# Logits of sliding-window softmax attention: two products over 128 rows against three products over 64 rows

## The chip, the cores and the metric

The kernel runs on one core of one Trainium2 chip. The metric is the device time of one execution in microseconds (us). The kernel before was timed three times: 2427.46, 2427.9 and 2433.88 us, median 2427.9 us. One more execution was recorded by the hardware profiler, and all rows of the trace below come from that one.

## The reference, cut to what matters

One decoder layer over 256 positions of width 2048: a SwiGLU feed-forward block, a pair of token mixers (retention and sliding-window softmax attention) fed by one projection, a second feed-forward block, a last RMS norm. The change concerns the logits of the softmax attention alone: 32 query heads of width 64, 8 key heads (four query heads share one), window and block of 128 positions.

```python
def swa_with_sinks(q, k, v, sinks):
    ...
    logits = jnp.einsum('bnqhgd,bnkhd->bnhgqk', qb, kb).astype(jnp.float32) * (d ** -0.5)
    ...
    logits = jnp.where(valid[None, :, None, None], logits, NEG_INF)
    ...
    probs = jax.nn.softmax(jnp.concatenate([logits, sink], axis=-1), axis=-1)[..., :-1]
    out = jnp.einsum('bnhgqk,bnkhd->bnqhgd', probs.astype(v.dtype), vb)
    return out.reshape(b, s, hq * d)
```

## The kernel before, in words

All large products are done in fp32r on TensorE with each operand split in two parts, a rounded part ("hi", written by a ScalarE cast) and what is left over ("lo", a VectorE subtraction). A product of activations and weights is three matmuls (lines 348 to 350): hi with hi, lo with hi, hi with lo, each 128 x 512 outputs wide. They go into the accumulators called `pa`. The weights arrive by DMA as `raw` and are split into `wh` and `wl` at lines 356 and 357.

The token mixing goes over the projection `w_in` in chunks of 512 columns (`in_chunk`). While the three matmuls of a chunk run, side work is fed between them: after every quarter of a chunk `gemm` calls `step()`, which advances a list `side` of generators by one. Softmax attention is such side work. A generator `window(pair)` handles two query heads (a pair); there are 16 pairs. Its first half is `window_weights` (logits, mask, exponentials), its second half `window_values` for the pair before (transposes of the weights, line 1251, and the products with the values, line 1267).

What the logits read is made ahead of them. `keys` holds, for each of the eight key heads, the hi part and the lo part with the head's 64 numbers twice, on partitions 0 to 63 and again on 64 to 127. `queries` holds for each pair two forms, one for each head: the head's hi part on its own half of the partitions, its lo part on the other half (lines 1316 to 1322, two ScalarE casts and two VectorE subtractions of 64 x 512 for each of two row blocks in each of four chunks). So one matmul over 128 partitions against hi keys gives hi times hi plus lo times hi, and a second against lo keys gives hi times lo plus lo times lo.

`window_weights` (from line 1189) writes the two heads' logits of the second row block, which see 256 keys, into one PSUM bank, and those of the first row block, which see 128 keys, into a second bank: eight matmuls for a pair (line 1202), four of 256 columns and four of 128. VectorE then reads the first bank once (line 1209, times the mask `pick`), adds two halves (line 1210), and reads the second bank once (line 1211). The banks come from the pool `psd` (`side_bank`), which has two.

The order of the instructions on TensorE, VectorE and ScalarE in this stretch is not the order of the code: a scheduler sets it from the dependencies and its own model of durations. The engines then work through their lists strictly in that order.

Of the kernel before, what the change touches and what calls it, by code (L numbers as in the profile page):

```python
# [9 lines left out]
F32 = mybir.dt.float32  # L10
F32R = mybir.dt.float32r
AF = mybir.ActivationFunctionType
ALU = mybir.AluOpType
# [3 lines left out]
P = 128  # L17
S = 256
# [12 lines left out]
QH, KVH, HD = 32, 8, 64  # L31
# [46 lines left out]
def layer_kernel(  # L78
# [22 lines left out]
    nc = tc.nc  # L101
# [16 lines left out]
    def nm(s):  # L118
        uid[0] += 1
        return f"{s}_{uid[0]}"  # L120
# [4 lines left out]
    def bank():  # L125
        return psm.tile([P, CH], F32, tag="ps", name=nm("ps"))

    def side_bank():
        return psd.tile([P, CH], F32, tag="pd", name=nm("pd"))

    def t512():
        return tmp.tile([P, CH], F32, tag="t512", name=nm("t"))
# [7 lines left out]
    def small(n, tag):  # L140
        return two.tile([P, n], F32, tag=tag, name=nm(tag))
# [218 lines left out]
    def pair_tile():  # L360
        return asp.tile([P, 2, CH], F32, tag="a", name=nm("a"))
# [46 lines left out]
    def gemm(act, w, col0s, KT=KD, ready=None):  # L408
        banks = [[acc_bank() for _ in range(NT)] for _ in col0s]
        for kb in range(KT // KB):  # L410
            gemm_part(act, w, col0s, banks, kb, KT, ready if kb == 0 else None)
            step()
        return banks
# [454 lines left out]
    banks, moved = {}, set()  # L868
# [104 lines left out]
    with tc.manual_schedule(engines=ORDERED):  # L973
# [21 lines left out]
        for _ in range(3):  # L995
# [8 lines left out]
            out=s2, in_=ssq.rearrange("p (t i) -> p t i", t=NT), axis=AX.X, op=ALU.add  # L1004
        )
        nc.vector.tensor_scalar(
            out=v2, in0=s2, scalar1=1.0 / D, scalar2=EPS, op0=ALU.mult, op1=ALU.add
# [6 lines left out]
            out=q2, in0=q2, scalar1=-0.5, scalar2=1.5, op0=ALU.mult, op1=ALU.add  # L1014
# [85 lines left out]
    for g, ks in enumerate(groups):  # L1100
# [7 lines left out]
        for i, n in enumerate(order):  # L1108
            if i < first_i:
                continue  # L1110
            at = i - first_i
# [25 lines left out]
    def in_chunk(c0, ready=None):  # L1137
        return gemm(held, wi, [c0], ready=ready)[0]
# [10 lines left out]
    keys = one.tile([P, 2, KVH, S], F32R, tag="x", name="keys")  # L1149
    b = in_chunk(O_SV, ready)  # L1150
    for t in range(NT):
        for g in range(2):
# [8 lines left out]
            for j in range(4):  # L1161
                js = slice(j * P, (j + 1) * P)
                nc.tensor.transpose(ps[:, js], kd[:, js], ident)
            hi, lo = (
                keys[:, i, g * 4 : g * 4 + 4, t * P : (t + 1) * P] for i in range(2)
            )
            p4 = ps.rearrange("p (h s) -> p h s", h=4)
# [5 lines left out]
    for t in range(NT):  # L1173
# [4 lines left out]
    queries = [  # L1178
        v.rearrange("p (j a s) -> p j a s", j=4, a=2)
        for v in (homes[:, : KD * P], other, homes[:, : KD * P], homes[:, KD * P :])  # L1180
    ]
# [3 lines left out]
    pick, causal, own = masks[:, : 2 * P], masks[:, 2 * P : 3 * P], masks[:, 3 * P :]  # L1185

    def twice(v):
        return v[:, None, :].broadcast_to([P, 2, v.shape[1]])

    def window_weights(pair):  # L1190


        kv = pair // 2
        both = pair_tile()
        lg, parts = both[:, :, :S], both[:, :, S:]
        banks = [side_bank(), side_bank()[:, :S]]
        of_t = [v.rearrange("p (i s) -> p i s", i=2) for v in banks][::-1]
        for i in range(2):
            qs = queries[pair // 4][:, pair % 4, i, :]
            for t in (1, 0):  # L1200
                for n in range(2):
                    nc.tensor.matmul(  # L1202
                        of_t[t][:, i, :],
                        qs[:, t * P : (t + 1) * P],
                        keys[:, n, kv, : (t + 1) * P],
                        start=n == 0,
                        stop=n == 1,
                    )
        nc.vector.tensor_mul(parts, of_t[1], twice(pick))
        nc.vector.tensor_add(lg[:, :, :P], parts[:, :, :P], parts[:, :, P:])  # L1210
        nc.vector.scalar_tensor_tensor(
            out=lg[:, :, P:], in0=of_t[0], scalar=HD**-0.5, in1=twice(causal),
            op0=ALU.mult, op1=ALU.add,
        )
        mx = small(4, "mx")
        m2 = mx.rearrange("p (i t) -> p i t", t=2)
        nc.vector.tensor_reduce(
            out=m2, in_=lg.rearrange("p i (t s) -> p i t s", t=2), axis=AX.X, op=ALU.max
        )
        sb = sink_b[:, 2 * pair : 2 * pair + 2]  # L1220
        nc.vector.tensor_tensor(
            out=m2, in0=m2, in1=sb[:, :, None].broadcast_to([P, 2, 2]), op=ALU.max
        )
        ng = small(4, "ng")
        nc.vector.tensor_scalar(out=ng, in0=mx, scalar1=-1.0, scalar2=None, op0=ALU.mult)
        se = small(4, "se")
        nc.vector.tensor_tensor(
            out=se.rearrange("p (i t) -> p i t", t=2),
            in0=ng.rearrange("p (i t) -> p i t", t=2),
            in1=sb[:, :, None].broadcast_to([P, 2, 2]),  # L1230
            op=ALU.add,
        )
        nc.scalar.activation(se, se, AF.Exp)
        sm = small(4, "sm")
        for i in range(2):
            for z in (2 * i, 2 * i + 1):
                seg = lg[:, i, z % 2 * P : (z % 2 + 1) * P]
                nc.scalar.activation(
                    seg, seg, AF.Exp, bias=ng[:, z : z + 1], accum_out=sm[:, z : z + 1]
                )  # L1240
        nc.vector.tensor_add(sm, sm, se)
        nc.vector.reciprocal(sm, sm)
        return lg, sm
# [46 lines left out]
    def window(pair):  # L1290
        held_lg = window_weights(pair)
        if pair > 4 and pair % 4 == 1:
            window_out(pair // 4 - 1)
        yield
        if before:
            window_values(*before.pop())
        before.append((pair, *held_lg))
        if pair == QH // 2 - 1:
            yield
            window_values(*before.pop())  # L1300
            yield
            window_out(pair // 4)
        yield

    for ci in range(4):
        b = in_chunk(O_SQ + ci * CH)
        for t in range(NT):
            u = t512()
            nc.any.tensor_copy(u, b[t])
            ps = bank()  # L1310
            for j in range(4):
                js = slice(j * P, (j + 1) * P)
                nc.tensor.transpose(ps[:, js], u[:, js], ident)
            q4 = queries[ci]
            p4 = ps.rearrange("p (j s) -> p j s", j=4)
            for a in range(2):
                here, there = (slice(c * HD, (c + 1) * HD) for c in (a, 1 - a))
                hi = q4[here, :, a, t * P : (t + 1) * P]
                nc.scalar.copy(hi, p4[here])
                nc.vector.tensor_sub(  # L1320
                    q4[there, :, a, t * P : (t + 1) * P], p4[here], hi.bitcast(F32)
                )
        side += [window(pair) for pair in range(ci * 4, ci * 4 + 4)]


# [1 line left out]
    for a, off in ((0, O_RQ), (1, O_RK)):  # L1327
        for ci in range(2):
            b = in_chunk(off + ci * CH)
            for t in range(NT):  # L1330
                u = t512()
                v = t512()
                p4 = b[t].rearrange("p (h a d) -> p h a d", h=4, a=2)
# [107 lines left out]
    for p in range(2):  # L1441
        sg = first if p == 0 else gates(p)
        c0s = [(2 * p + i) * CH for i in range(2)]
        for g, a, w in ((1, a_swa, w_swa_branch), (0, a_ret, w_ret_branch)):
            banks = gemm(a, w[0], c0s)
# [109 lines left out]
```

## Time and profile before

| | us |
|---|---|
| median of three timed runs | 2427.9 |
| lowest, highest | 2427.46, 2433.88 |
| the profiled execution, as timed | 2425.96 |
| its span, first to last instruction | 2424.2 |
| TensorE matmul busy in the span | 2394.7 |
| VectorE, ScalarE busy | 1707.3, 1182.5 |

An engine's busy time is the time in which at least one of its instructions is running. Matmuls overlap in the pipeline, so the duration of one matmul (0.39 us for 512 columns) is longer than the distance between the starts of two that follow each other; what a matmul costs in a stream is read from the starts. Weight loads (PEld) are recorded apart from the matmuls (PE). Where the records show two matmuls starting within 0.03 us of each other, the next distance is longer, and only the sum over such a place can be used.

### The profile page before, as it was taken

How to read it: one execution, taken by the hardware profiler on the slowest of the kernel's cores; microseconds unless marked ns; L12 is line 12 of the kernel's file. 1: busy time of each engine (PE TensorE's matmuls, PEld its weight loads, DVE VectorE, ACT ScalarE, POOL GpSimd, SP SyncE). 2: the span in 40 equal slices, each digit the busy share in tenths (PEclk: the TensorE clock that was granted, in tenths of full speed). 3: DMA queues.
4: the chain of work that ended last, by engine and by line, in shares of the span. 5: the costliest groups of instructions: out<-in, count | busy, mean ns of one | idle time of the engine just before them, and what ended most of it. 6: DMA issues, size and time to landing. Idle time of an engine off the chain costs nothing.

```text
span 2424.2 us, 28881 instructions
## 1 busy us (share of the span) xinstructions
PE 2394.7 (99%) x10916; PEld 1981.0 (82%) x10916; DVE 1707.3 (70%) x2497; ACT 1182.5 (49%) x1596; POOL 8.3 (0%) x19
## 2 busy tenths in 40 slices
PE   7999999999999999999999999999999999999998
PEld 5887888888888888888888788888888888888886
DVE  7878787778877688886666776768565555545656
ACT  6644554444546455454444444456444444444544
POOL 0000000000000000000000000000000000000000
PEclk9999999999999999999999999999999999999999
DMA  9887678888876666566677777755666666665563
GB/s 372 329 300 302 210 273 334 333 315 319 309 287 217 242 223 224 209 244 209 243 261 255 248 260 272 266 191 191 211 242 224 226 226 235 234 224 191 185 199 122
DMA packets 244543, 603.32 MB, mean 249 GB/s; under 512 B 9810, under 2 KB 10194, under 8 KB 224818
## 3 DMA queue, kind: packets, MB, share of 16 engines
q1 hardware_dynamic: 242850, 591.61, 68.6%
q0 software_dynamic: 1552, 9.87, 1.0%
q8 instruction: 85, 1.39, 0.2%
q14 instruction: 56, 0.45, 0.1%
HBM read 597.22 MB, written 4.22 MB: 248 GB/s over the span
## 4 chain that ended last, share of the span: by engine, by line
PE 95%; DMA 2%; DVE 2%; issue 0%; ACT 0%; SPq 0%; DVEq 0%; ACTq 0%
PE pa L350 28%; PE pa L349 28%; PE pa L348 28%; DMA slot<-in_w_ada_dram 2%; PE pa L724 1%; PE ps L466 1%; PE pd L348 1%; PE pd L350 1%; PE pd L349 1%; PE pd L1267 1%; PE pd L1202 1%; DVE wl L357 0%; PE pd L1251 0%; DMA x_sb<-in_x_dram 0%; DVE slot L227 0%
## 5 line engine op out<-in xcount | busy, mean ns | idle before, releaser
L357 DVE TENSOR_TENSOR wl<-raw,wh 128x1024 fp32r<-128x1024 f32 (+1 forms) x784 | 942.2, 1206 | 591.2 <-ACT wh L356 587.0
L356 ACT CAST wh<-raw 128x1024 fp32r<-128x1024 f32 (+1 forms) x784 | 815.0, 1040 | 1025.7 <-PE pa L349 972.3
L348 PE MATMUL pa<-wh,hh 128*128 128x512 f32 x2014 | 788.4, 391 | 0.9 <-ACT wh L356 0.9
L349 PE MATMUL pa<-wh,hl 128*128 128x512 f32 x2014 | 786.8, 391 | 0.0
L350 PE MATMUL pa<-wl,hh 128*128 128x512 f32 x2014 | 726.8, 392 | 0.0
L348 PEld LDWEIGHTS pa<-wh,hh 128*128 128x128 f32 x2014 | 378.2, 188 | 78.7 <-ACT wh L356 1.3
L349 PEld LDWEIGHTS pa<-wh,hl 128*128 128x128 f32 x2014 | 378.2, 188 | 76.9
L350 PEld LDWEIGHTS pa<-wl,hh 128*128 128x128 f32 x2014 | 376.2, 188 | 76.2
L349 PE MATMUL pa<-wh,a 128*128 128x512 f32 x992 | 384.2, 389 | 1.2 <-DVE a L389 1.2
L348 PE MATMUL pa<-wh,a 128*128 128x512 f32 x992 | 367.2, 390 | 1.1 <-ACT wh L356 0.9
L350 PE MATMUL pa<-wl,a 128*128 128x512 f32 x992 | 367.0, 390 | 0.6 <-DVE wl L357 0.6
L348 PEld LDWEIGHTS pa<-wh,a 128*128 128x128 f32 x992 | 185.9, 188 | 41.4 <-ACT wh L356 1.8
L349 PEld LDWEIGHTS pa<-wh,a 128*128 128x128 f32 x992 | 186.2, 188 | 40.6 <-DVE a L389 2.1
L350 PEld LDWEIGHTS pa<-wl,a 128*128 128x128 f32 x992 | 185.8, 188 | 40.2 <-DVE wl L357 1.9
L227 DVE CUSTOM_DVE_ANT_0 slot<-slot,cact 128x1024 f32<-128x1024 f32 (+1 forms) x126 | 182.4, 1475 | 18.9 <-DMA slot<-in_w_ada_dram 18.7
L227 DVE CUSTOM_DVE_ANT_0 raw<-raw,cact 128x512 f32<-128x512 f32 (+1 forms) x260 | 166.9, 695 | 24.0 <-DMA raw<-in_w_ada_dram 22.9
L389 DVE TENSOR_TENSOR a<-slot,a 128x512 fp32r<-128x512 f32 x124 | 84.8, 685 | 4.9 <-ACT a L388 4.9
L388 ACT CAST a<-slot 128x512 fp32r<-128x512 f32 x124 | 76.4, 618 | 5.3 <-PE pa L350 5.2
L467 ACT COPY slot<-ps 128x512 f32<-128x512 f32 x75 | 41.4, 586 | 35.2 <-PE ps L466 35.0
L348 PE MATMUL pd<-wh,hh 128*128 128x512 f32 x144 | 56.1, 391 | 1.1 <-DVE slot L947 1.1
L349 PE MATMUL pd<-wh,hl 128*128 128x512 f32 x144 | 56.1, 390 | 0.0
L350 PE MATMUL pd<-wl,hh 128*128 128x512 f32 x144 | 51.2, 392 | 0.0
(237 smaller groups left out, 1398.7 us busy)
## 6 DMA issues: line engine op xcount, KB each, us to landing
raw<-in_w_ffn_gu_dram SPq DMA_DIRECT2D x148, 1024.0 KB, 4.9
raw<-in_w_in_dram SPq DMA_DIRECT2D x104, 1024.0 KB, 5.1
raw<-in_w_ffn_down_dram SPq DMA_DIRECT2D x88, 1024.0 KB, 5.0
slot<-in_w_ada_dram SPq DMA_DIRECT2D x78, 1024.0 KB, 7.6
raw<-in_w_ada_dram SPq DMA_DIRECT2D x64, 1024.0 KB, 4.8
raw<-in_w_ffn_gu_dram SPq DMA_DIRECT2D x25, 768.0 KB, 7.5
raw<-in_w_swa_branch_dram SPq DMA_DIRECT2D x16, 1024.0 KB, 5.1
raw<-in_w_ret_branch_dram SPq DMA_DIRECT2D x16, 1024.0 KB, 5.2
```

What stands on the lines that cost most here:

```text
L227: nc.vector.tensor_tensor_reduce(out=w[:, at], in0=w[:, at], in1=cact[:, at], scale=1.0, scalar=0.0, op0=ALU.mult, op1=ALU.add, accum_out= ...
L348: nc.tensor.matmul(ps, ah[:, j, ts], wh[:, j, :], start=first, stop=False)
L349: nc.tensor.matmul(ps, al[:, j, ts], wh[:, j, :], start=False, stop=False)
L350: nc.tensor.matmul(ps, ah[:, j, ts], wl[:, j, :], start=False, stop=last)
L356: nc.scalar.copy(hi, src)
L357: nc.vector.tensor_sub(lo, src, hi.bitcast(F32))
L388: nc.scalar.copy(hi, v)
L389: nc.vector.tensor_sub(lo, v, hi.bitcast(F32))
L466: nc.tensor.transpose(ps[:, j * P : (j + 1) * P], src_of(j), ident)
L467: nc.any.tensor_copy(dest, ps[:, : n * P])
L724: nc.tensor.matmul(banks[t], a[:, j, t * P : (t + 1) * P], wt[:, j, :], start=(kb, hs[0], n) == (0, 0, 0), stop=(kb, hs[-1], n) == (KD // ...
L1202: nc.tensor.matmul(of_t[t][:, i, :], qs[:, t * P : (t + 1) * P], keys[:, n, kv, : (t + 1) * P], start=n == 0, stop=n == 1,)
```

## The change

The logits of a head become three matmuls over that head's 64 partitions: hi queries with hi keys, lo with hi, hi with lo. The product lo with lo is no longer formed. The heads of a pair sit on opposite halves of the partitions and are written by turns in the code; each head gets a PSUM bank of its own, 256 columns for the second row block and 128 beside them for the first. A pair has twelve matmuls instead of eight. VectorE reads each bank twice, so four instructions instead of two. The queries are stored as a hi tile and a lo tile, each over all 128 partitions: one cast and one subtraction of 128 x 512 where there were two of each of 64 x 512.

```diff
-        banks = [side_bank(), side_bank()[:, :S]]
-        of_t = [v.rearrange("p (i s) -> p i s", i=2) for v in banks][::-1]
+        banks = [side_bank() for _ in range(2)]
+        terms = ((0, 0), (1, 0), (0, 1))
+        for t, at in ((1, slice(0, S)), (0, slice(S, S + P))):
+            for n, (of_q, of_k) in enumerate(terms):
+                for i in range(2):
+                    here = slice(i * HD, (i + 1) * HD)
+                    nc.tensor.matmul(
+                        banks[i][:, at],
+                        queries[pair // 4][here, pair % 4, of_q, t * P : (t + 1) * P],
+                        keys[here, of_k, kv, : (t + 1) * P],
+                        start=n == 0,
+                        stop=n == len(terms) - 1,
+                    )
         for i in range(2):
-            qs = queries[pair // 4][:, pair % 4, i, :]
-            for t in (1, 0):
-                for n in range(2):
-                    nc.tensor.matmul(
-                        of_t[t][:, i, :],
-                        qs[:, t * P : (t + 1) * P],
-                        keys[:, n, kv, : (t + 1) * P],
-                        start=n == 0,
-                        stop=n == 1,
-                    )
-        nc.vector.tensor_mul(parts, of_t[1], twice(pick))
+            nc.vector.tensor_mul(parts[:, i, :], banks[i][:, :S], pick)
+            nc.vector.scalar_tensor_tensor(
+                out=lg[:, i, P:], in0=banks[i][:, S : S + P], scalar=HD**-0.5, in1=causal,
+                op0=ALU.mult, op1=ALU.add,
+            )
         nc.vector.tensor_add(lg[:, :, :P], parts[:, :, :P], parts[:, :, P:])
-        nc.vector.scalar_tensor_tensor(
-            out=lg[:, :, P:], in0=of_t[0], scalar=HD**-0.5, in1=twice(causal),
-            op0=ALU.mult, op1=ALU.add,
-        )
...
-            for a in range(2):
-                here, there = (slice(c * HD, (c + 1) * HD) for c in (a, 1 - a))
-                hi = q4[here, :, a, t * P : (t + 1) * P]
-                nc.scalar.copy(hi, p4[here])
-                nc.vector.tensor_sub(
-                    q4[there, :, a, t * P : (t + 1) * P], p4[here], hi.bitcast(F32)
-                )
+            hi, lo = (q4[:, :, a, t * P : (t + 1) * P] for a in range(2))
+            nc.scalar.copy(hi, p4)
+            nc.vector.tensor_sub(lo, p4, hi.bitcast(F32))
```

The scheduler's order on TensorE, at the first pair. `pd` is a side bank, `pa` an accumulator of the projection; L1202 is the logits' line in both kernels, and 128x256 or 128x128 is the size of the output. Before, in a row:

```order
L349 MATMUL pa_6438<-wh_6543,hl_4048 128x512
L1202 MATMUL pd_6477<-keys,homes_6263 128x256 x2
L1202 MATMUL pd_6478<-keys,homes_6263 128x128 x2
L350 MATMUL pa_6437<-wl_6544,hh_4047 128x512
L350 MATMUL pa_6438<-wl_6544,hh_4047 128x512
```

And after, ten of the pair's twelve, where pd_6473 is the bank of the first head and pd_6474 that of the second:

```order
L349 MATMUL pa_6434<-wh_6545,hl_4048 128x512
L1202 MATMUL pd_6473<-keys,homes_6263 128x256
L1202 MATMUL pd_6474<-keys,homes_6263 128x256
L1202 MATMUL pd_6473<-keys,homes_6263 128x256
L1202 MATMUL pd_6474<-keys,homes_6263 128x256
L1202 MATMUL pd_6473<-keys,homes_6263 128x128
L1202 MATMUL pd_6474<-keys,homes_6263 128x128
L1202 MATMUL pd_6473<-keys,homes_6263 128x128
L1202 MATMUL pd_6474<-keys,homes_6263 128x128
L1202 MATMUL pd_6473<-keys,homes_6263 128x128
L1202 MATMUL pd_6474<-keys,homes_6263 128x128
L350 MATMUL pa_6433<-wl_6546,hh_4047 128x512
```

Here the halves do alternate; the same holds, with two doubled rows, for the second pair.

TensorE again, at the third pair, the second of its two runs of logits. Before:

```order
L348 MATMUL pa_6684<-wh_6823,hh_4047 128x512
L349 MATMUL pa_6684<-wh_6823,hl_4048 128x512
L1202 MATMUL pd_6722<-keys,homes_6263 128x128 x4
L350 MATMUL pa_6684<-wl_6824,hh_4047 128x512
L348 MATMUL pa_6683<-wh_6871,hh_4047 128x512
L349 MATMUL pa_6683<-wh_6871,hl_4048 128x512
```

After (L1252 is the transposes of `window_values`, line 1251 before):

```order
L349 MATMUL pa_6687<-wh_6833,hl_4048 128x512
L350 MATMUL pa_6687<-wl_6834,hh_4047 128x512
L1202 MATMUL pd_6726<-keys,homes_6263 128x256 x3
L1202 MATMUL pd_6726<-keys,homes_6263 128x128 x3
L1252 MATMUL pd_6797<-small_c,a_6578 128x128 x4
L348 MATMUL pa_6688<-wh_6833,hh_4047 128x512
```

Before, a run is one row block of both heads; after, a run is all six matmuls of one head, in one bank and on one half of the partitions, and the other head's six stand 30 rows further up. From the third pair to the sixteenth the two heads' runs stay apart in this way, by other distances, and two of the 28 runs are cut into five and one. With the three runs of the first two pairs (2, 10 and 12 matmuls) that makes 33 runs; before there are 34, all but four of them of four matmuls.

VectorE at the third pair, before:

```order
L1209 TENSOR_TENSOR a_6720<-pd_6721,slot_6259 128x2x256
L1320 TENSOR_TENSOR other<-ps_6674,other 64x4x128
L1210 TENSOR_TENSOR a_6720<-a_6720 128x2x128
L357 TENSOR_TENSOR wl_6889<-raw_6869,wh_6888 128x1024
L1320 TENSOR_TENSOR other<-ps_6663,other 64x4x128
L1320 TENSOR_TENSOR other<-ps_6674,other 64x4x128
L1211 SCALAR_TENSOR_TENSOR a_6720<-pd_6722,slot_6259 128x2x128
```

After:

```order
L1210 TENSOR_TENSOR a_6724<-pd_6725,slot_6259 128x256
L1319 TENSOR_TENSOR other<-ps_6680,other 128x4x128
L1211 SCALAR_TENSOR_TENSOR a_6724<-pd_6725,slot_6259 128x128
L357 TENSOR_TENSOR wl_6888<-raw_6885,wh_6887 128x1024
L357 TENSOR_TENSOR wl_6905<-raw_6885,wh_6904 128x1024
L1210 TENSOR_TENSOR a_6724<-pd_6726,slot_6259 128x256
L1211 SCALAR_TENSOR_TENSOR a_6724<-pd_6726,slot_6259 128x128
```

The reading of a bank is split by heads, and the queries' subtraction (L1320 before, L1319 after) stands half as often.

## Rows read from the trace of the kernel before

**Rows 1.** The page, busy time of each engine over the span
```profile
PE 2394.7 (99%) x10916; PEld 1981.0 (82%) x10916; DVE 1707.3 (70%) x2497; ACT 1182.5 (49%) x1596; POOL 8.3 (0%) x19
```

**Rows 2.** Windows: stretch, length, busy us (instructions) by engine, clock, DMA share, GB/s
```profile
845.00:1095.00 250.00, 250.00 (x1340) 213.74 (x1339) 206.34 (x437) 128.84 (x273) 1.59 (x3) 1.00 0.63 222
```

**Rows 3.** Timeline, TensorE: start, us, engine, line, operation, tiles, shapes, count
```profile
857.47 0.39 PE L349 MATMUL pa<-wh,hl 128*128 128x512 f32 x1
857.69 0.63 PE L1202 MATMUL pd<-keys,homes 128*128 128x256 f32 x4
858.16 0.39 PE L350 MATMUL pa<-wl,hh 128*128 128x512 f32 x1
858.39 0.40 PE L348 MATMUL pa<-wh,hh 128*128 128x512 f32 x1
```

**Rows 4.** Timeline, TensorE, around four logits of 128 columns
```profile
862.49 0.56 PE L1202 MATMUL pd<-keys,homes 128*128 128x128 f32 x4
862.89 0.45 PE L349 MATMUL pa<-wh,hl 128*128 128x512 f32 x1
863.17 0.62 PE L350 MATMUL pa<-wl,hh 128*128 128x512 f32 x2
```

**Rows 5.** Timeline, weight loads and matmuls of the three start-up transposes
```profile
9.81 0.18 PEld L200 LDWEIGHTS ps<-small_c,t 48*128 48x128 f32 x1 [3.67 <-DMA small_c<-in_consts_dram]
10.07 0.18 PEld L201 LDWEIGHTS ps<-small_c,t 128*128 128x128 f32 x1
10.48 0.18 PEld L202 LDWEIGHTS ps<-small_c,t 16*128 16x128 f32 x1 [0.22 <-issue]
...
10.08 0.47 PE L201 MATMUL ps<-small_c,t 128*128 128x128 f32 x1
10.48 0.28 PE L202 MATMUL ps<-small_c,t 16*128 16x16 f32 x1
```

**Rows 6.** Timeline, TensorE, two transposes of one shape
```profile
18.14 0.77 PE L899 MATMUL ps<-small_c,t 128*128 128x128 f32 x2 [2.26 <-ACT t L892]
```

**Rows 7.** Timeline, TensorE, around a transpose with 16 output rows
```profile
451.17 0.39 PE L349 MATMUL pa<-wh,hl 128*128 128x512 f32 x1
451.40 0.27 PE L291 MATMUL ps<-small_c,modc 128*16 128x128 f32 x1
451.42 0.71 PE L350 MATMUL pa<-wl,hh 128*128 128x512 f32 x2
451.97 0.40 PE L348 MATMUL pa<-wh,hh 128*128 128x512 f32 x1
```

**Rows 8.** Groups by shape: count, busy us, mean ns, idle before; or ns min/median/max
```profile
L1209 DVE TENSOR_TENSOR a<-pd,slot 128x512 f32<-128x512 f32 x16 | 11.0, 687 | 0.4
L1211 DVE SCALAR_TENSOR_TENSOR a<-pd,slot 128x256 f32<-128x256 f32 x16 | 6.8, 422 | 6.3 <-PE pd L1202 6.2
L1320 DVE TENSOR_TENSOR homes<-ps,homes x12: 683/686/694, 843.2 to 942.5; 64x512 fp32r<-64x512 f32 x12
L1320 DVE TENSOR_TENSOR other<-ps,other x4: 684/686/694, 878.5 to 882.8; 64x512 fp32r<-64x512 f32 x4
L389 DVE TENSOR_TENSOR a<-slot,a 128x512 fp32r<-128x512 f32 x124 | 84.8, 685 | 4.9 <-ACT a L388 4.9
L1319 ACT CAST homes<-ps x12: 579/581/584, 842.6 to 941.4; 64x512 fp32r<-64x512 f32 x12
L1319 ACT CAST other<-ps x4: 579/582/586, 877.9 to 880.6; 64x512 fp32r<-64x512 f32 x4
```

**Rows 9.** Timeline, start: matmuls over one row, and their weight loads
```profile
4.53 0.62 PE L188 MATMUL pa<-c,ones 1*128 1x512 f32 x1
4.95 0.62 PE L189 MATMUL pa<-c,ones 1*128 1x512 f32 x1
...
4.53 0.33 PEld L189 LDWEIGHTS pa<-c,ones 1*128 1x128 f32 x1
4.96 0.33 PEld L188 LDWEIGHTS pa<-c,ones 1*128 1x128 f32 x1
```

## The prediction

> **What bounds the kernel now.** I read the page first. TensorE is busy for 2394.7 of 2424.2 us [rows 1], which alone says little, since a busy matmul row need not be a row at full pace. So I took the windows of the stretch in which the change works: the first logits start at 850, the last values end near 1089 us, and from 845 to 1095 TensorE is busy for 250.00 of 250 us at a granted clock of 1.00, the 2.4 GHz level, VectorE for 206.34, ScalarE for 128.84 [rows 2]. The reader is to see that nothing else ever holds TensorE up there: what the change costs or saves on TensorE moves the end one for one, and what it does on VectorE and ScalarE has 43.7 and 121.2 us of idle time to disappear in. The third view was the timeline of TensorE alone, because it gives the distance between starts, which is what a matmul costs in a stream.
>
> **What a small matmul costs.** Matmuls of 512 columns start 0.23 us apart. Four logits matmuls of 256 columns stand between two of them: they start at 857.69, the next large one at 858.16, and it is followed at the usual distance [rows 3]. So the four cost 0.47 us, 0.118 each. Four of 128 columns take 0.40 to the next start, and that next one then takes 0.28 in place of 0.23, so 0.45 in all, 0.113 each [rows 4]. Half the columns save almost nothing: both run at the pace at which weights are loaded, not at that of the columns.
>
> **Part 1, the count.** Before: 16 pairs with four of either kind, 16 x (0.47 + 0.45) = 14.7 us. After: six of either kind per pair, 96 x 0.118 + 96 x 0.113 = 22.2 us, if a matmul over 64 rows costs what one over 128 costs. It does unless its weights load faster, and the start-up transposes show loads of 48, 128 and 16 rows that all take 0.18 us [rows 5]. I take +7.4 us. From below: if half the rows loaded in half the time, the 128-column ones would be bound by their columns, 0.23 x 128/512 = 0.057 us, and the sum would be 96 x 0.118 + 96 x 0.057 = 16.8, +2.1 us.
>
> **Part 2, opposite halves.** The code alternates the halves, so that two heads could stream at once. But the order, which the scheduler sets, does so for two pairs of sixteen; in the other fourteen a run is six matmuls of one head on one half, and the other head's run stands some large matmuls away. So at most 24 matmuls can overlap, worth at most 12 x 0.115 = 1.4 us. No row of before has two halves at work. Bounds 0 and -1.4, I take the middle, -0.7.
>
> **Part 3, changing the shape of the array's use.** Each of the 33 runs now stands between instructions over 128 rows, so TensorE goes from 128 rows to 64 and back 66 times; before never, in this stretch. What does a change cost? The nearest rows are the start-up transposes. The 128-row one starts at 10.08, the 16-row one at 10.48, 0.40 apart, and the weight load of the second sat idle for 0.22 us behind nothing that the profile shows, until just before the first was done [rows 5]. Two transposes of one shape, at the same slow pace, start 0.77 - 0.47 = 0.30 apart [rows 6]. So the change cost 0.10 there. The other way: in the middle of the full-pace stream, a transpose with 16 output rows goes by between 128-row matmuls; from 451.17 to 451.97 there are three 512-column matmuls (3 x 0.23) and it, so it cost 0.11, what a small matmul costs anyway, and nothing for the change [rows 7]. That one changes the columns of the array in use, not its rows. Bounds per change: 0 by that row, 0.22 by the idle load. I take 0.10, the row that changes rows as this kernel does, unhalved although the start-up runs at the slower pace (0.42 us per 512 columns [rows 9]), since it does not show what the time consists of: 66 x 0.10 = +6.6 us; ends 0 and 14.5.
>
> The Trainium skill says in TensorEngine Tiling (Array Packing), under Key Properties, that changing the tiling mode, not just the tile, drains the TensorE; it gives no time. The start-up transposes [rows 5] agree with it and the 16-row one [rows 7] does not: with it the sum has the term of part 3, without it the sum stops at part 1 and 2.
>
> **Part 4, VectorE and ScalarE.** Reads of the banks: before 687 + 422 ns a pair. After, two of 128 x 256 at 422 and two of 128 x 128, which by the same slope (265 ns per 256 columns) I estimate at 290: 1424 ns, +0.32 us a pair, +5.0 us. The queries: 16 subtractions of 64 x 512 at 686 ns become 8 of 128 x 512, and half as many partitions were not cheaper: line 389 takes 685 on 128 [rows 8]. So -5.5 us on VectorE, and 8 casts of 0.58 less on ScalarE, -4.7 us. The net, near zero and negative, lies under TensorE's 250 us without a gap. If that cover went, it would be through a bank: with two side banks, head two's run, or the transposes after it, wait for VectorE to have read the other bank, twice now. The six waits of VectorE for the logits (6.3 us in all [rows 8]) say that VectorE comes to the bank first as often as not. I take 0, and allow +2 us; a matmul that waits in TensorE's list holds up all large ones behind it.
>
> **The sum.** 7.4 - 0.7 + 6.6 = +13.3 us on the profiled execution, 2425.96 + 13.3 = 2439.3, its 1.8 us outside the span unchanged. The median of the runs shown is 1.9 us above that execution, so 2427.9 + 13.3 = 2441.2; I forecast 2441. With 0.05 to 0.22 us per change, and part 2 between its ends, it is +9 to +22, 2437 to 2450.
>
> **The rivals.**
> *A change of rows is free.* Then +6.0 to +7.4 us, 2434 to 2435. For it the 16-row transpose in the stream [rows 7], against it the start-up [rows 5]; it decides below some 0.02 us per change. This lies just under 0.3%, which is 7.3 us and about what a measurement of this kernel tells from none.
> *Not slower: half-height weights load in half the time, and a change is free.* The mechanism sits in the 96 matmuls of 128 columns, whose price falls from 0.113 to 0.057. Then +2.1 - 0.7 = +1.4, with the 256-column ones still at 0.118; 2429. Against it the equal loads [rows 5], taken at the slow pace where something else might set 0.18. It decides from a price below about 0.08 for each.
> *The halves do run side by side everywhere*, as the change says: 192 matmuls in 96 places, 96 x 0.115 = 11.0 against 14.7, -3.7 us, 2424. The order speaks against it, since the runs of the two halves are large matmuls apart. Even then it stays within 0.3%; faster by more would need half of the 14.7 us to go.
> *Loads on one half do not run ahead.* If in a run on one half each weight load waits for the matmul before it, every logits matmul bears a load in the open. What that is worth: after the transpose the two matmuls of line 350 take 451.42 to 451.97, 0.55 for 2 x 0.23, so 0.09 [rows 7]. 192 x 0.09 = 17 more, +31 us, 2459. Against it: the start-up matmuls over a single row have their next load start together with the matmul before it, and keep an even 0.42 apart [rows 9]. The Trainium skill has the rule for it in TensorE: Matmul & The Clock Gate, Part 3, The mechanism: a load overlaps a matmul in flight only where the row group differs. These loads [rows 9] and all of the 128-row stream contradict it.
>
> **How the numbers follow.** Forecast 0.56; change free 0.20; half-time loads 0.12; side by side 0.04; loads in the open 0.08. Slower by over 0.3%: the forecast, the last rival, and a third of the free change, since its upper end sits on the line: 0.70 in round numbers. Faster by over 0.3%: 0.02, for something in the fourth that I do not see. Within: 0.28. The range 2430 to 2452 holds the forecast with its ends and 2 us of bank waits, and the free change; it leaves out the loads in the open, the side by side, and half of the half-time loads. The forecast's own range is 2437 to 2450.
>
> **What would show it.** In the profile after: 192 matmuls on line 1202, their six-runs 0.69 us long from start to start plus some 0.1 at either side; the weight load of each run's first matmul, and that of the first large one after it, starting late by that much; TensorE's stretch of side work longer by 13 us, with the stages before and after it unchanged; alternate starts within a few hundredths only in the first two pairs. I am wrong if the six-runs are bordered at the ordinary 0.23 us, if six take much less than 0.69, or if TensorE waits for a side bank.

## The result, and the profile after

The changed kernel takes 2450.03 us (median of six runs, 2445.09 to 2453.46) against 2430.7 us for the kernel before (six runs): a ratio of 1.0081, 95% interval 1.0069 to 1.0092, or +17 to +22 us of 2430. The forecast was 2441, slower, in a range from 2430 to 2452.

The profiled execution of the changed kernel took 2452.41 us, at the upper end of its runs, and part of the 26 us between the two profiled executions lies outside the change. So I compare inside the stretch, between two large matmuls, one ahead of the first logits and one behind the last, with the same other matmuls between them in both kernels. Before, then after:

```profile
847.63 0.39 PE L349 MATMUL pa<-wh,hl 128*128 128x512 f32 x1
1097.39 0.40 PE L349 MATMUL pa<-wh,hl 128*128 128x512 f32 x1
...
853.57 0.39 PE L349 MATMUL pa<-wh,hl 128*128 128x512 f32 x1
1119.94 0.39 PE L349 MATMUL pa<-wh,hl 128*128 128x512 f32 x1
```

The stretch grows from 249.8 to 266.4 us, by 16.6. Of the rest, 5.9 us lie ahead of it and 4 behind. There the execution after shows TensorE idle for 1.6 us and a clock of 0.83 from 205 to 215 us, and the same idle time and a clock of 0.79 from 1363 to 1371; that of before shows no idle time and 1.00 in both windows.

The page's first row, and the same stretch by windows, as [rows 1, 2] for before:

```profile
PE 2416.2 (99%) x10980; PEld 1991.6 (81%) x10980; DVE 1702.4 (69%) x2520; ACT 1179.3 (48%) x1589; POOL 8.3 (0%) x19
```
```profile
845.00:1115.00 270.00, 270.00 (x1423) 224.35 (x1422) 204.42 (x464) 127.64 (x269) 1.58 (x3) 1.00 0.60 209
```

64 matmuls more, VectorE and ScalarE a little less busy, and TensorE again without an idle moment at a granted clock of 1.00. What grew is the time between its starts. The timeline of TensorE (start, duration, line, operation, tiles, shapes, count), first at the second pair, whose twelve matmuls go by turns, then at the second head of the third pair, six on one half; and under it the weight loads of the latter moment:

```profile
862.80 0.39 PE L350 MATMUL pa<-wl,hh 128*128 128x512 f32 x1
863.12 0.90 PE L1202 MATMUL pd<-keys,homes 64*128 64x256 f32 x12
863.96 0.49 PE L348 MATMUL pa<-wh,hh 128*128 128x512 f32 x1
864.29 0.39 PE L349 MATMUL pa<-wh,hl 128*128 128x512 f32 x1
...
887.82 0.39 PE L349 MATMUL pa<-wh,hl 128*128 128x512 f32 x1
888.04 0.39 PE L350 MATMUL pa<-wl,hh 128*128 128x512 f32 x1
888.36 0.90 PE L1202 MATMUL pd<-keys,homes 64*128 64x256 f32 x6
889.19 0.66 PE L1252 MATMUL pd<-small_c,a 128*128 128x128 f32 x4
```
```profile
887.82 0.19 PEld L350 LDWEIGHTS pa<-wl,hh 128*128 128x128 f32 x1
888.36 0.75 PEld L1202 LDWEIGHTS pd<-keys,homes 64*128 64x128 f32 x6 [0.35 <-issue]
889.19 0.42 PEld L1252 LDWEIGHTS pd<-small_c,a 128*128 128x128 f32 x4
```

In the stream, the weights of a matmul are loaded while the one before it runs. Here the load for the first logits sits idle for 0.35 us behind "issue", which is nothing that the profile shows, and starts only at 888.36, together with its matmul, 0.32 after the start of the last large one instead of 0.23. The six take 0.83 us to the next start, where 0.69 was worked out; all 26 runs of six take 0.82 to 0.84. The twelve by turns take 0.84, no longer than six on one half, and the large matmul after them 0.33 in place of 0.23. So a run costs 0.09 ahead of it, 0.14 within and 0.10 behind, some 0.34 us over its places of 0.115 each; and two matmuls on opposite halves share one place. VectorE's reads came out as estimated [rows 8], the 128-column one at 279 ns where I had 290:

```profile
L1210 DVE TENSOR_TENSOR a<-pd,slot 128x256 f32<-128x256 f32 x32 | 13.4, 419 | 6.7 <-PE pd L1202 6.6
L1211 DVE SCALAR_TENSOR_TENSOR a<-pd,slot 128x128 f32<-128x128 f32 x32 | 8.9, 279 | 0.0
```

### The profile page after: what moved, and what is told of

Read it like the earlier page. It is cut to its first block, busy times and chain, and to the rows that moved or that the text cites. A ratio compares the mean times of both kernels' runs of the same rounds, so it can differ in the third digit from the quotient of the medians.

```text
span 2450.6 us, 29039 instructions
## 1 busy us (share of the span) xinstructions
PE 2416.2 (99%) x10980; PEld 1991.6 (81%) x10980; DVE 1702.4 (69%) x2520; ACT 1179.3 (48%) x1589; POOL 8.3 (0%) x19
## 4 chain that ended last, share of the span: by engine, by line
PE 94%; DMA 3%; DVE 2%; issue 1%; ACT 0%; SPq 0%; DVEq 0%; ACTq 0%
PE pa L350 28%; PE pa L349 28%; PE pa L348 28%; DMA slot<-in_w_ada_dram 2%; PE pa L724 1%; PE ps L466 1%; PE pd L348 1%; PE pd L349 1%; PE pd L350 1%; PE pd L1202 1%; PE pd L1268 1%; DVE wl L357 1%; PE pd L1252 0%; DMA x_sb<-in_x_dram 0%; DMA raw<-in_w_ada_dram 0%
```

## The experiments

The theory: 33 runs x 0.34 + 192 x 0.115 - 12 shared places x 0.115 = 31.9 us where there were 14.7, +17 us. All differences below are the measured ratio less one, times 2430 us, with the interval. In some places the trace of the one profiled execution is added, as the time between two large matmuls, one ahead of the first logits and one well behind the last (847.63 and 1164.09 us before), with the same other matmuls between them in every kernel; I call this the long stretch.

**1. All 128 rows, everything else left.** Both heads get the sum of the two heads' logits.

```diff
-                    here = slice(i * HD, (i + 1) * HD)
+                    here = slice(0, P)
```

> The changed kernel with all twelve logits matmuls of a pair over 128 partitions in place of 64 (so each head gets the sum of both heads' products; the order of the instructions, the banks, the reads and the query split stay those of the changed kernel, word for word). Theory (border): what the change costs beyond its 64 more matmuls is paid where TensorE goes from 128 rows to 64 and back, about 0.34 us per run of logits; without the 64 rows only the count is left, 64 x 0.115 = +7.4 us against the kernel before, about 2438, and the six-runs sit 0.69 us from start to start with 0.23 at either side. Rival (reads and order): the rest comes from the split reads, the banks or the new order; then it stays near +19, about 2450.

Measured: ratio 1.0031 (1.0020 to 1.0041), +7.5 us (4.9 to 10.0). The same order, banks, reads and query split as the changed kernel, row for row, and two thirds of the loss are gone. A six-run of it and what follows:

```profile
908.62 0.40 PE L349 MATMUL pa<-wh,hl 128*128 128x512 f32 x1
908.86 0.80 PE L1202 MATMUL pd<-keys,other 128*128 128x256 f32 x6
909.49 0.44 PE L350 MATMUL pa<-wl,hh 128*128 128x512 f32 x1
909.77 0.39 PE L348 MATMUL pa<-wh,hh 128*128 128x512 f32 x1
```

It starts 0.24 after the large matmul and takes 0.63, the next 0.28: 0.69 us above the stream, against 1.03. The count is worth 7.5 us and the 64 rows the rest. The rival, reads and order, is out.

**2. Two terms, so eight matmuls as before, on 64 rows.** The product of lo queries and hi keys is left out.

```diff
-        terms = ((0, 0), (1, 0), (0, 1))
+        terms = ((0, 0), (0, 1))
```

> The changed kernel without the product of lo queries and hi keys: eight matmuls per pair as in the kernel before, each over 64 rows (28 runs of four on one half, two runs of eight by turns). Theory (border): a run costs 0.34 + 0.115 per place, 30 x (0.34 + 4 x 0.115) = 24.0 us against 14.7 before, +9.3 us, about 2440; a four-run and its borders take 0.80 us. Rival (per matmul): each 64-row matmul costs 0.17 wherever it stands, as the six-runs' 1.03 us divided by six; then a four-run with its borders takes 0.68, and the sum is +5.7, about 2436. Rival (count alone): no change against before, about 2430.

Measured: 1.0033 (1.0020 to 1.0046), +8.0 us (4.9 to 11.2). With no matmul added it is slower, so count alone falls. The times don't part the other two (9.3 and 5.7 both lie inside), the trace does:

```profile
911.61 0.39 PE L350 MATMUL pa<-wl,hh 128*128 128x512 f32 x1
911.92 0.68 PE L1202 MATMUL pd<-keys,other 64*128 64x256 f32 x4
912.53 0.50 PE L348 MATMUL pa<-wh,hh 128*128 128x512 f32 x1
912.86 0.39 PE L349 MATMUL pa<-wh,hl 128*128 128x512 f32 x1
```

0.08 ahead, 0.61 for the four, 0.10 behind: 0.79, where the price per run says 0.80 and the price per matmul 0.68.

**3. By turns for every pair.** The twelve are chained, and their banks come from two pools where both are free at once.

```diff
-        banks = [side_bank() for _ in range(2)]
+        banks = [bank(), acc_bank()]
...
+                    if last is not None:
+                        tc.add_manual_dep(mm.ins, last.ins.name, ...)
+                    last = mm
```

> The changed kernel with the twelve matmuls of each pair chained so that they issue by turns on the two halves, and with the two banks taken from the transposes' pool and the accumulators' pool, so that 18 runs are left, 16 whole twelves but for two that are cut. Theory (border and overlap): two matmuls on opposite halves share one place; 18 x 0.34 + 96 x 0.115 = 17.2 us against 14.7 before, +2.5 us, about 2433; a twelve-run takes 0.84 us from its start to the next. Rival (no overlap; the fast twelve-run of the profile is an accident of its place): 18 x 0.34 + 192 x 0.115 = 28.2, +13.5 us, about 2444.

Measured: 1.0014 (1.0003 to 1.0025), +3.4 us (0.7 to 6.1), as the theory has it. Here the two banks have different names, so the timeline keeps the matmuls apart (from the start of a run on; `ps` and `pa` are the two heads' banks):

```profile
888.11 0.40 PE L350 MATMUL pa<-wl,hh 128*128 128x512 f32 x1
888.43 0.38 PE L1203 MATMUL ps<-keys,homes 64*128 64x256 f32 x1
888.44 0.38 PE L1203 MATMUL pa<-keys,homes 64*128 64x256 f32 x1
888.66 0.27 PE L1203 MATMUL ps<-keys,homes 64*128 64x256 f32 x1
888.66 0.27 PE L1203 MATMUL pa<-keys,homes 64*128 64x256 f32 x1
888.77 0.28 PE L1203 MATMUL ps<-keys,homes 64*128 64x256 f32 x1
...
889.26 0.50 PE L348 MATMUL pa<-wh,hh 128*128 128x512 f32 x1
```

The two heads start within 0.01 us of each other. The first place takes 0.22 and those after it 0.11: the load in the open at the head of a run is to be seen here by itself.

**4. The order and banks of 3, both heads on the lower half.** The second head of a pair gets the first one's logits.

```diff
-                    here = slice(i * HD, (i + 1) * HD)
+                    here = slice(0, HD)
```

> As the kernel by turns with 18 runs, same order and same banks, but both heads read the lower half of the partitions (so the second head of a pair gets the first one's logits). Theory (overlap needs opposite halves): each matmul has a place of its own, 18 x 0.34 + 192 x 0.115 = 28.2 us, +13.5 against before, about 2444, 11 us above the kernel by turns; a twelve-run takes about 1.5 us. Rival (it is the alternation of the two banks that lets matmuls overlap): as the kernel by turns, about 2433.

Measured: 1.0045 (1.0031 to 1.0058), +10.9 us (7.5 to 14.1). A run of twelve, its start and what follows it:

```profile
888.53 0.38 PE L1203 MATMUL ps<-keys,homes 64*128 64x256 f32 x1
888.75 0.28 PE L1203 MATMUL pa<-keys,homes 64*128 64x256 f32 x1
888.87 0.28 PE L1203 MATMUL ps<-keys,homes 64*128 64x256 f32 x1
888.99 0.28 PE L1203 MATMUL pa<-keys,homes 64*128 64x256 f32 x1
...
889.85 0.27 PE L1203 MATMUL pa<-keys,homes 64*128 64x128 f32 x1
890.05 0.43 PE L1278 MATMUL pd<-slot,t 128*128 128x64 f32 x2
```

1.52 us against 0.83: opposite halves let two matmuls share a place, not two banks. Within the run starts are 0.11 to 0.12 apart, the pace of full-height matmuls.

**5. By turns, with the banks left in the side pool.** The edit of 3 without its first line.

> The changed kernel with the twelve matmuls of a pair chained by turns, and its two banks left in the side pool: the first matmul of most pairs then goes alone and eleven follow, 35 runs in place of 18, with nearly the same sharing of places. Theory (border, 0.34 us per run): against the kernel by turns with 18 runs 17 more runs, +5.8 us, and some six places lost where a lone matmul has no partner, +0.7; about 2440 where that one is 2433.4, +10 against before. Rival (what is left of the price is per matmul, not per run): within 1 us of the kernel with 18 runs, 2433 to 2434.

Measured: 1.0185 (1.0171 to 1.0199), +45 us (41 to 48). Neither was right. Windows of 5 us (busy us and instructions by engine, then the clock):

```profile
1010.00:1015.00 5.00, 5.00 (x31) 4.01 (x30) 2.21 (x2) 2.41 (x3) 0.00 (x0) 1.00 0.65 247
1015.00:1020.00 5.00, 2.93 (x16) 2.14 (x14) 4.37 (x12) 3.73 (x13) 0.00 (x0) 1.00 0.63 210
1020.00:1025.00 5.00, 1.89 (x9) 1.89 (x10) 4.82 (x16) 0.00 (x0) 0.00 (x0) 0.66 0.22 40
1025.00:1030.00 5.00, 5.00 (x17) 3.87 (x17) 2.39 (x8) 0.00 (x0) 0.00 (x0) 0.65 0.45 173
```

And what stood in VectorE's list there (the bracket is the idle time before, and what ended it):

```profile
1020.18 0.69 DVE L227 CUSTOM_DVE_ANT_0 raw<-raw,cact 128x512 f32<-128x512 f32 x1 [0.68 <-DMA raw<-in_w_ada_dram]
...
1022.64 0.42 DVE L1272 TENSOR_TENSOR t<-pd,t 128x256 f32<-128x256 f32 x1
...
1023.11 2.39 PE L1278 MATMUL pd<-slot,t 128*128 128x64 f32 x10 [4.44 <-DVE t L1272]
```

The scheduler's new order has TensorE waiting for a VectorE instruction (L1272, a subtraction that readies the softmax weights for the products with the values), which stands behind four passes over a row that has just landed. That the lone first matmul, which takes one bank and waits for the other, led to this order was not shown. TensorE idles 4.44 us, and the granted clock of the windows in and behind the gap is 0.66 and 0.65, partly at the 1.2 GHz level; ten matmuls whose row is 1.22 us long elsewhere in this run take 2.39. From 950 to 1100 us the idle time comes to 16 us in all. An estimate from the trace: the long stretch is 42 us longer than before; TensorE waits for 17 us of it, is busy for some 27 us at the lower level, which at half the pace loses some 13, and the borders were expected at 10.

**6. The reads alone.** The kernel before with one bank per head and the four split reads.

```diff
-        banks = [side_bank(), side_bank()[:, :S]]
+        banks = [side_bank() for _ in range(2)]
...
-        nc.vector.tensor_mul(parts, of_t[1], twice(pick))
+        for i in range(2):
+            nc.vector.tensor_mul(parts[:, i, :], banks[i][:, :S], pick)
+            nc.vector.scalar_tensor_tensor(
+                out=lg[:, i, P:], in0=banks[i][:, S : S + P], ...)
...
```

> The kernel before, its eight matmuls over 128 partitions and its query split kept, with one bank per head and the four split reads on VectorE of the changed kernel. Theory: VectorE has 43 us of idle time in the stretch and TensorE never waits for a bank, so nothing: 2429.4, within 0.1%. Rival (banks): VectorE frees a bank later and TensorE waits, 0.2 us per pair, +3 us or more.

Measured: 1.0002 (0.9994 to 1.0011). Nothing, as expected.

**7. Twice the changes of rows.** The changed kernel in its own order, with the second of each head's six matmuls over 128 rows; that term sums both heads.

```diff
+                    if (t, n) == (1, 1):
+                        here = slice(0, P)
```

> The changed kernel with one of the six matmuls of each head (lo queries by hi keys, 256 columns, second in the run) over all 128 partitions, so that its term sums both heads; order, banks and count stay those of the changed kernel. Each run now changes rows twice more, some 60 changes more in all. Theory (the price is per change of rows, 0.34 us for going and coming back): 30 x 0.34 = +10 us above the changed kernel, about 2460, +30 against before. Rival (the price is per run, paid once where the logits meet the large matmuls): no more than the changed kernel, about 2450.

Measured: 1.0121 (1.0105 to 1.0136), +29 us (25 to 33), about 10 above the changed kernel, with nothing added but changes, and two shared places lost in the first two pairs. The run that stood at 888.36 above:

```profile
887.67 0.39 PE L350 MATMUL pa<-wl,hh 128*128 128x512 f32 x1
887.99 1.29 PE L1204 MATMUL pd<-keys,homes 64*128 64x256 f32 x6
889.21 0.66 PE L1254 MATMUL pd<-small_c,a 128*128 128x128 f32 x4
```

1.22 us in place of 0.83, so 0.39 for the added going and coming back, a little over 0.34. The price is per change of rows, wherever it stands, not per run.

**8. Fewer weight loads.** The kernel before, with hi and lo keys of the first row block as one matmul of 256 columns; VectorE adds the two parts with one more read.

```diff
-            for t in (1, 0):
-                for n in range(2):
-                    nc.tensor.matmul(of_t[t][:, i, :], qs[:, t * P : (t + 1) * P], keys[:, n, kv, : (t + 1) * P], ...)
+            for n in range(2):
+                nc.tensor.matmul(of_t1[:, i, :], qs[:, P:], keys[:, n, kv, :], start=n == 0, stop=n == 1)
+            nc.tensor.matmul(of_t0[:, i], qs[:, :P], keys[:, :, kv, :P], start=True, stop=True)
...
+        nc.vector.scalar_tensor_tensor(out=lg[:, :, P:], in0=of_t0[:, :, 1], ..., in1=lg[:, :, P:], ...)
```

> The kernel before (128 partitions, its query split) with the first row block's two matmuls of 128 columns, hi keys and lo keys, put into one of 256 columns against both; VectorE adds the two halves with a second read of the bank (16 more instructions of 0.42 us). Theory: small matmuls are bound by their weight loads, so 64 of 0.113 us become 32 of 0.118, -3.5 us, about 2426. Rival: the matmul takes as long as its columns, or the added read is felt; then 2429 to 2431.

Measured: 2425.85 us, 0.9984 (0.9975 to 0.9993), -3.9 us (-6.1 to -1.7): faster than both kernels. Its first row block, as [rows 4] for before:

```profile
883.35 0.40 PE L1205 MATMUL pd<-keys,homes 128*128 128x256 f32 x2
883.58 0.39 PE L349 MATMUL pa<-wh,hl 128*128 128x512 f32 x1
883.81 0.40 PE L350 MATMUL pa<-wl,hh 128*128 128x512 f32 x1
```

0.23 us for two where four took 0.45 [rows 4]; the added 16 reads (6.7 us) lie in VectorE's idle time almost whole. TensorE now waits once, 0.3 us, for the splitting of weights on VectorE (line 357), where before it never waited in this part; and in the trace the long stretch is 1.9 us shorter, not 3.5, so the gain is shown better than its size.

## Why the prediction was right, and where its sizes were off

*What bounds the stretch*: right. TensorE had no gap before or after, and experiment 6 puts 16 times 0.32 us more on VectorE without a trace in the time.

*Part 1, the count, +7.4*: right. Experiment 1 measures it as +7.5 (4.9 to 10.0). The equal loads at 48, 128 and 16 rows [rows 5] carried it: full height or half, the small matmuls keep their 0.11 to 0.12 us (experiment 4). With this the rival of half-time loads is out.

*Part 2, opposite halves, -0.7*: the lower bound was the right value. The 24 matmuls that the order left by turns do share their places, all of them: -1.4. That the order, not the code, decides how many these are was the point; where the order is forced the same matmuls cost 16 us less than in the changed kernel (experiment 3 against the result). The sums of terms differ by nearly as much: 17.2 us against 31.9.

*Part 3, the change of rows, +6.6*: the mechanism was right, the size too small, and this is the term that was off. I took 0.10 us per change from the start-up transposes [rows 5, 6]; 0.34 per run is 0.17 per change, 66 x 0.17 = 11.2 (0.39 for the round trip in experiment 7 would be a little more). What I left out can be read in the rows after: the wait for the matmul before (0.09 going in) was in my number, but the next weight load, which here does not run ahead, then lies in the open too (0.22 for the first place instead of 0.11), and both come again going out. The start-up pair [rows 6] I compared with has its own load in the open, so the comparison took that part away. Rows in which a price is already paid on both sides don't show it.

That [rows 7] showed a transpose with 16 output rows passing for nothing is not contradicted: it changes the columns in use, and its 0.11 us is what a small matmul costs anyway. The Trainium skill says in TensorEngine Tiling (Array Packing), under Key Properties, that a change of tiling mode drains TensorE. The rows agree for a change of rows, at 0.34 us for going and coming back, and show no cost for the change of columns [rows 7].

*Part 4*: right. I allowed 2 us for a wait at a bank, and there is none in the changed kernel. Experiment 5 shows what another order from the scheduler can do: there TensorE waits 17 us, 9.9 of them for the subtraction on line 1272 and 2.5 for a bank that VectorE has yet to read (line 1221), and the clock falls as well. No allowance of mine covered that.

*The sum*: with the measured sizes 7.4 - 1.4 + 11.2 = +17.2 us, against +17 to +22 measured and +16.6 in the stretch of the trace. So the terms account for the stretch, and what the timed runs show beyond it need not come from the change. The experiments bear the sizes out in the same way: the long stretch is longer than before by 7.7, 8.9, 2.8 and 13.7 us in experiments 1 to 4, where the sums say 7.4, 9.3, 2.5 and 13.5.

The forecast of 2441 lies 9 us low. Part 3 is 4.6 of that, less 0.7 for part 2; 2.8 are the baseline, 2427.9 us in the three runs shown and 2430.7 in all six; some 2 lie outside the sum. The measured 2450 is the very end of the forecast's own range, which came that far by 0.22 us per change; the 2 us for bank waits that carry the wider range to 2452 stand for something that did not happen.

*The rivals*: a free change fell by experiments 1, 2 and 7. The halves side by side everywhere did not happen in the changed kernel; where it was made to happen, the kernel lost 3.4 us rather than gaining 3.7, since 18 borders remain. Loads in the open on one half fell by experiment 4: within its runs the loads take 0.18 us each and matmuls start 0.11 to 0.12 apart, so a load runs beside a matmul on its own half. The Trainium skill says in TensorE: Matmul & The Clock Gate, Part 3, The mechanism, that a load overlaps a matmul in flight only where the row group differs. Experiment 4 does not agree, and the measurement decides.

## What to carry to other kernels

Before cutting small matmuls to half height, count the places where TensorE goes over to the other height and back in the order that the scheduler makes, not in the code; by an estimate from 0.34 us for each round trip and 0.115 for a place, a run must share three places to pay for it, if the cut adds no matmuls. Turning two matmuls into one of more columns was the better direction here, where 128 columns cost 0.113 us and 256 cost 0.118 and VectorE had time for the extra read: -3.9 us in experiment 8. A stall in front of TensorE can cost more than its length: in experiment 5 the clock fell during the 4.44 us gap, and ten matmuls behind it took 2.39 us in place of 1.22.

## What the runs showed of the hardware that was not expected

A weight load for 64 rows of 128 columns takes 185 ns where one for 128 rows takes 188 (line 1202, after and before), so half the height saves nothing; this was expected, but only from the slower start-up rows [rows 5]. Not expected was the rest. Going over to 64 rows and back costs 0.34 us, and 0.39 inside a run (experiment 7). Six 64-row matmuls on one half and twelve by turns on both take the same 0.83 to 0.84 us. After a gap of 4.44 us the granted clock stayed below full in the next 5 us window as well (0.65).
